# Prompt weights' transpose in the bank of the value sums, new places for the score blocks, and part of the sixth output tile ahead, in a hybrid Mamba‑2 / differential‑attention step

## The chip, the cores and the metric

The kernel runs on one core of a Trainium2 chip. The metric is the device time of one launch in microseconds (us); lower is better.

## The reference

One inference step of a two-layer diffusion backbone serves 128 prompt (context) tokens and 512 latent tokens, T = 640 together, at model width D = 1024. Layer 0 mixes tokens with a bidirectional Mamba‑2 scan, layer 1 with differential attention; after each of them comes a gated FFN with hidden width 2816 and a width-3 convolution, and a final RMSNorm ends the trunk. Every sub-layer is normalised, modulated by a conditioning vector and added back with a gate. The change touches layer 1's attention alone, which is, cut to what matters (shapes in comments, not code of the kernel):

```python
q, k, v = split(h @ w_qkv)                 # 8 heads, each two maps of 64 and values of 128
q, k = rope_2d(q), rope_2d(k)              # on latent tokens only
# prompt: 128 queries x 128 prompt keys; latent: 512 queries x (512 latent + 128 cached keys)
a0, a1 = softmax(q0 @ k0.T / 8), softmax(q1 @ k1.T / 8)
o = (a0 - lam * a1) @ v                    # per head
o = rms(o) * subg * (1 - LAM_INIT)         # norm over each head's 128 values
x = x + gate * (concat(o) @ w_ao)
```

The new keys and values of the prompt tokens are outputs too. All of it is float32.

## The kernel before

**Precision and dense tiles.** A float32 matrix product is made from two float32r parts of each operand: wh·xh, wh·xl and wl·xh. Activations lie transposed, features on 128 partitions and 640 tokens in the row. A *dense tile* is 128 output features; it goes over the inner dimension in steps k of 128, and in each step three products are made for token columns "A" (256) and "B" (384). So a step is 6 matmuls and a tile with 8 steps 48. `dense_many` (L158) issues them and calls `hook()` after every step.

**Weights.** `weight_units` lists all weight tiles in the order of their use. `nextw` takes the next one; it also starts the DMA three tiles ahead (`raw`, 4 buffers, SP's queue) and the split of the next tile: `whi` by ScalarE (helper `act`, L95) and `wlo = raw - whi` by VectorE (helper `tt`, L101). In attention there are 3 buffers of each.

**Tasks.** `hook()` advances a list of generators. A task that yields n comes back n hooks later, that is n×6 dense matmuls later. So the places of all other TensorE work among the dense matmuls are numbers in `yield`s. The framework's scheduler then decides the order on ScalarE and VectorE by priority; `high_priority()` raises that of the instructions in its block.

**PSUM.** Pool `psd` has three buffers of two banks: dense tiles (`q`, `k`, `v`, `po`) and the pairs of score tiles (`sl`, prompt: `sp`) take them in turn. Two more banks have the tags "m" (`wt`, `vt`, `ms`, `op` and, before the change, `wpt`) and "y" (`ov`).

**A head.** For each of 8 heads `attention` runs the dense tiles q, k, v. The head's scores start during its own v tile and go on in the next head's q, k and v, so tiles of one head and scores of the head before run together:
- `att_head`: prompt scores `sp`, their softmax and combination `wp`; a yield; four blocks of 128 latent queries, each 12 matmuls `sl` (both maps), a reduction `sm` on VectorE (L1079), two exponentials `e` on ScalarE, then `combine`: reciprocal, a scaling of the second map's `e` on ScalarE, and `w = e0*s + e1` on VectorE (L98). Between blocks there is a yield from a small table.
- `att_v` transposes v (`vt`, L1015) and splits it.
- `att_tail` transposes `wp` (`wpt`, L1128); then for each of five key chunks four transposes `wt` (L1145), their split `wTh` (ScalarE) and `wTl` (VectorE), and three value sums `ov` of the chunk before; then the prompt's sum `op`, squares `osq`, the row sums `ms`, nine small VectorE operations from `rs_v` (L178) to `rs_y` (`rsqrt`), and the factor back over the partitions: by DMA for heads 0 to 6, by matmul `obc` for head 7.

**The output projection.** `project_out` makes output tiles 0 to 4 over the first six heads (36 matmuls each); heads 6 and 7 finish beside it. `project_last` then adds heads 6 and 7 to tiles 0 to 4 (12 matmuls each; their weights come grouped in two units), and runs output tiles 5, 6 and 7 over all eight heads, columns A first and then B, each followed by gate, residual (`xr`) and squares for the next norm.

Of the kernel before, what the change touches and what calls it, by code (L numbers as in the profile page):

```python
# [9 lines left out]
F32 = mybir.dt.float32  # L10
# [3 lines left out]
AF = mybir.ActivationFunctionType  # L14
ALU = mybir.AluOpType
# [3 lines left out]
P = 128  # L19
D = 1024  # L20
KT = D // P
# [24 lines left out]
class Step:  # L46
# [111 lines left out]
    def dense_many(self, tiles, ks, h, parts, n=None, i0=0):  # L158


        n = n or len(ks)
        for i, k in enumerate(ks, i0):
            for ps, (hi, lo), m in tiles:
                st, sp = i == 0, i == n - 1
                wh, wl = hi[:, i * m:(i + 1) * m], lo[:, i * m:(i + 1) * m]
                for wt, x, s0, s1 in ((wh, h[k][0], st, False), (wh, h[k][1], False, False), (wl, h[k][0], False, sp)):
                    for p in parts:
                        c0, c1 = HALF[p]
                        self.mm(ps[:m, COL0[p] + c0:COL0[p] + c1], wt, x[:, c0:c1], s0, s1)
            self.hook()  # L170
# [119 lines left out]
    def project_last(self, h, ks, g, nextnorm, ks_last=None, parts="AB"):  # L290


        self.norm_begin()
        for i in range(KT - 3):
            ps = self.dense_ps("po")
            n = len(ks) * P
            j = i % (1024 // n) if ks_last else 0
            if j == 0:
                w = self.nextw()
            self.dense(ps, [t[:, j * n:(j + 1) * n] for t in w], ks, h)  # L300
            for hf in "AB":
                self.gate_add(i, ps, g, hf)
                self.norm_sq(i, hf)
        ks = ks_last or ks
        if self.modtask:
            self.drain(self.modtask)
        ws = [(self.dense_ps("po"), self.nextw(), i) for i in range(KT - 3, KT)]
        for hf in parts:
            for grp in ((ws[0:1], ws[1:3]) if hf == "B" else (ws[0:1], ws[1:2], ws[2:3])):
                self.dense_many([(ps, w, P) for ps, w, i in grp], ks, h, hf)  # L310
                for ps, w, i in grp:
                    self.gate_add(i, ps, g, hf)
                    self.norm_sq(i, hf)
            self.normt[hf] = self.add(nextnorm(hf), 3)
# [753 lines left out]
    def att_head(self, hd, qp, kp, qs, k, vs, o, pool):  # L1068


        nc = self.nc
        (qh, ql, i), (kh, kl, j) = qs, k
        lows = i, j
        half = [slice(64 * m, 64 * m + 64) for m in range(2)]

        def softmax(s, n, m, st):
            e = self.slot("f", f"e{m}", bufs=NF)
            with self.tc.high_priority():
                nc.vector.tensor_reduce(st[:, m:m + 1], s, AX.X, ALU.max, negate=True)  # L1079
                self.held["exp"] = self.act(e[:, :n], s, AF.Exp, bias=st[:, m:m + 1], accum_out=st[:, 2 + m:3 + m])  # L1080
            return e

        def stats():
            return pool.tile([P, 8], F32, tag="sm", name="sm", bufs=3)

        def combine(w, n, e0, e1, st):
            nc.vector.reciprocal(st[:, 4:6], st[:, 2:4])
            self.tt(st[:, 5:6], st[:, 5:6], self.nlam, ALU.mult)
            self.act(e1[:, :n], e1[:, :n], AF.Copy, scale=st[:, 5:6])
            self.stt(w, e0[:, :n], st[:, 4:5], e1[:, :n], ALU.mult, ALU.add)  # L1090

        r = self.psd.tile([P, 1024], F32, tag="d", name="sp")
        for m, hf in enumerate(half):
            self.mm(r[:, 512 * m:512 * m + TP], qp[hf], kp[hf], True, True)
        st = stats()
        em = [softmax(r[:, 512 * m:512 * m + TP], TP, m, st) for m in range(2)]
        yield 2
        last = hd == 7
        w = pool.tile([P, TP], F32, tag="wp", name="wp", bufs=1)
        combine(w, TP, *em, st)  # L1100
        yield 3 if last else 5 if hd else 3
        ws = []
        for b in range(4):
            qb = slice(b * P, (b + 1) * P)
            rs = [self.psd.tile([P, 1024], F32, tag="d", name="sl") for _ in range(2)]
            gate = [*self.held.values(), *lows]
            for j, (x, kk) in enumerate(((qh, kh), (qh, kl), (ql, kh))):
                for c0 in (0, 320):
                    for r, hf in zip(rs, half):
                        i = self.mm(r[:, 192 + c0:192 + c0 + 320], x[hf, qb], kk[hf, c0:c0 + 320], j == 0, j == 2)  # L1110
                        if j == 0:
                            self.hold(i, gate)
            st = stats()
            em = [softmax(r[:, 192:832], T, m, st) for m, r in enumerate(rs)]
            yield 2
            wb = pool.tile([P, T], F32, tag="w", name=f"w{b}", bufs=8)
            combine(wb, T, *em, st)
            ws.append(wb)
            if b < 3:
                yield {0: (3, 2, 2), 6: (2, 2, 2), 7: (1, 1, 1)}.get(hd, (4, 4, 4))[b]  # L1120
        self.tails[hd] = self.add(self.att_tail(hd, w, ws, vs, o, pool), 1 if last else 4)

    def att_tail(self, hd, w, ws, vs, os_, pool):

        nc = self.nc
        vh, vl, vp = vs
        pm = self.bank("m", "wpt")
        nc.tensor.transpose(pm[:, :P], w, self.ident)  # L1128
        wpT = pool.tile([P, TP], F32, tag="wpT", name="wpT", bufs=1)
        self.act(wpT, pm[:, :P], AF.Copy)  # L1130
        yield 1
        py = self.bank("y", "ov")
        o = self.slot("f", f"o{hd}", bufs=NF)
        os_.append(o)

        def av(kc, hi, lo, gate):
            self.hold(self.mm(py, vh[:, kc, :], hi, kc == 0, False), [gate])
            self.mm(py, vh[:, kc, :], lo, False, False)
            self.mm(py, vl[:, kc, :], hi, False, kc == NCH - 1)

        prev = None
        for kc in range(NCH):
            pm = self.bank("m", "wt")
            for b in range(4):
                nc.tensor.transpose(pm[:, b * P:(b + 1) * P], ws[b][:, kc * P:(kc + 1) * P], self.ident)  # L1145
            hi = pool.tile([P, TS], F32R, tag="wTh", name="wTh", bufs=2)
            lo = pool.tile([P, TS], F32R, tag="wTl", name="wTl", bufs=2)
            self.act(hi, pm, AF.Copy)
            gate = self.tt(lo, pm, hi.bitcast(F32), ALU.subtract)
            if prev:  # L1150
                av(kc - 1, *prev)
            prev = hi, lo, gate
            yield 1 if hd == 7 else 2
        av(NCH - 1, *prev)
        self.act(o[:, :TS], py, AF.Copy)
        pm = self.psm.tile([P, 512], F32, tag="m", name="op")
        self.mm(pm[:, :TP], vp, wpT, True, True)
        self.act(o[:, TS:], pm[:, :TP], AF.Copy)
        yield 1
        sq = self.slot("sq", "osq", bufs=1)  # L1160
        self.act(sq, o, AF.Square)
        yield 2
        if hd == 7:
            bc = yield from self.rms_bcast(lambda: self.wide("obc"), [sq], 0, T, P, 4)
        else:
            bc = yield from self.rms_spread(pool, [sq], P, 9)
        self.stt(o, o, self.sg[:, hd // 7:hd // 7 + 1], bc[:, :T], ALU.mult, ALU.mult)

    def attention(self, h, nextnorm, pool):
# [8 lines left out]
        for hd in range(8):  # L1178
            q, qp = self.att_evac(self.next_tile(h, "q"), hd, "q", pool)
            k, kp = self.att_evac(self.next_tile(h, "k"), hd, "k", pool)  # L1180
            nc.sync.dma_start(self.a["kout"][hd], kp)
            q = self.att_q(q, hd, pool)
            k = self.att_k(k, hd, pool)
            vs = []
            tk.append(self.add(self.att_head(hd, qp, kp, q, k, vs, o, pool), 1 if hd == 7 else 4))
            self.add(self.att_v(self.next_tile(h, "v"), hd, vs, pool), 1)
            if hd:
                self.drain(tk[hd - 1])
# [25 lines left out]
    def weight_units(self):  # L1214
        a = self.a
        u = [(a["w_dt"], 512)]
# [18 lines left out]
        for hd in range(8):  # L1235
# [3 lines left out]
        per = 1024 // (D - c)  # L1239
        u += [(a["w_ao"][i:j, :, c:].rearrange("i p c -> p i c"), (j - i) * (D - c))  # L1240
              for i in range(0, KT - 3, per) for j in (min(i + per, KT - 3),)]
        u += [(a["w_ao"][i], D) for i in range(KT - 3, KT)]
        u += ffn(1)
        return u

# [135 lines left out]
```

## Time and profile before

| what | value |
|---|---|
| median of 3 runs | 1879.43 us (1876.5 to 1879.79) |
| the profiled execution's own time | 1880.65 us |
| its span | 1878.9 us, 32832 instructions |
| TensorE (PE) busy | 1838.2 us, 98% |
| PE's weight loads (PEld) | 1741.9 us, 93% |
| VectorE (DVE) busy | 1369.5 us, 73% |
| ScalarE (ACT) busy | 952.9 us, 51% |
| mean granted TensorE clock | 0.995 |

The profile shows one execution. A timeline row gives start, duration, engine, line, operation and, in brackets, the idle time just before it with what ended it. A group gives the busy sum, the mean duration in ns and the idle time. The table of waits gives, for each kind of instruction and releaser, the idle sum, the count and the longest. The windows table gives busy time, granted clock (PEclk) and DMA share of each stretch. All helpers' instructions carry the helper's line (L95 ScalarE, L98 and L101 VectorE, L104 matmul), so they are told apart by the names of their tiles.

### The profile page before, as it was taken

How to read it: one execution, taken by the hardware profiler on the slowest of the kernel's cores; microseconds unless marked ns; L12 is line 12 of the kernel's file. 1: busy time of each engine (PE TensorE's matmuls, PEld its weight loads, DVE VectorE, ACT ScalarE, POOL GpSimd, SP SyncE). 2: the span in 40 equal slices, each digit the busy share in tenths (PEclk: the TensorE clock that was granted, in tenths of full speed). 3: DMA queues.
4: the chain of work that ended last, by engine and by line, in shares of the span. 5: the costliest groups of instructions: out<-in, count | busy, mean ns of one | idle time of the engine just before them, and what ended most of it. 6: DMA issues, size and time to landing. Idle time of an engine off the chain costs nothing.

```text
span 1878.9 us, 32832 instructions
## 1 busy us (share of the span) xinstructions
PE 1838.2 (98%) x13322; PEld 1741.9 (93%) x13322; DVE 1369.5 (73%) x2637; ACT 952.9 (51%) x1745; POOL 0.2 (0%) x4
## 2 busy tenths in 40 slices
PE   7999999999999999999999999999999999999997
PEld 5899999999999999999999988888899999999996
DVE  5699999999658999974555877788777543553554
ACT  3489687878336441441443656566445432431441
POOL 0000000000000000000000000000000000000000
PEclk9999999999999999999999999999999999999998
DMA  9835243436624556532222212111122222122211
GB/s 337 266 121 147 97 147 109 140 115 202 199 80 142 185 180 221 181 103 91 68 68 78 79 40 65 58 50 48 61 88 89 69 79 80 63 72 89 64 40 57
DMA packets 79679, 209.74 MB, mean 112 GB/s; under 512 B 9276, under 2 KB 16040, under 8 KB 79400
## 3 DMA queue, kind: packets, MB, share of 16 engines
q1 hardware_dynamic: 78952, 207.13, 33.5%
q8 instruction: 104, 1.70, 0.4%
q10 hardware_dynamic: 576, 0.52, 0.1%
q14 instruction: 47, 0.39, 0.1%
HBM read 201.66 MB, written 5.96 MB: 111 GB/s over the span
## 4 chain that ended last, share of the span: by engine, by line
PE 91%; DVE 4%; ACT 3%; DMA 1%; issue 1%; SPq 0%; DVEq 0%; ACTq 0%
PE up L104 31%; PE po L104 25%; PE z L104 6%; PE x L104 5%; PE st L104 5%; PE bc L104 3%; PE yp L104 3%; PE q L104 2%; PE v L104 2%; PE k L104 1%; PE modrow L104 1%; PE sl L104 1%; PE in L104 1%; ACT whi L95 1%; ACT e L95 1%; PE ov L104 1%
## 5 line engine op out<-in xcount | busy, mean ns | idle before, releaser
L95 ACT ACTIVATE whi<-raw 128x1024 fp32r<-128x1024 f32 (+3 forms) x227 | 234.2, 1033 | 387.2 <-PE po L104 239.6
L101 DVE TENSOR_TENSOR wlo<-raw,whi 128x1024 fp32r<-128x1024 f32 (+2 forms) x226 | 269.2, 1192 | 172.2 <-ACT whi L95 165.1
L98 DVE SCALAR_TENSOR_TENSOR xr<-po,mod,xr 128x256 f32<-128x256 f32 (+2 forms) x231 | 89.2, 433 | 162.0 <-PE po L104 161.8
L104 PE MATMUL po<-mh,whi 128*128 128x256 f32 (+1 forms) x704 | 167.8, 310 | 0.0
L104 PE MATMUL po<-ml,whi 128*128 128x256 f32 (+1 forms) x704 | 167.5, 310 | 0.0
L104 PE MATMUL po<-mh,wlo 128*128 128x256 f32 (+1 forms) x704 | 167.3, 310 | 0.0
L104 PE MATMUL up<-h11h,wlo 128*128 128x256 f32 (+1 forms) x656 | 149.4, 309 | 0.0
L104 PE MATMUL up<-h01h,wlo 128*128 128x256 f32 (+1 forms) x656 | 149.4, 308 | 0.0
L104 PE MATMUL up<-h01h,whi 128*128 128x256 f32 (+1 forms) x656 | 149.3, 308 | 0.0
L104 PE MATMUL up<-h01l,whi 128*128 128x256 f32 (+1 forms) x656 | 149.3, 308 | 0.0
L104 PE MATMUL up<-h11l,whi 128*128 128x256 f32 (+1 forms) x656 | 149.3, 308 | 0.0
L104 PE MATMUL up<-h11h,whi 128*128 128x256 f32 (+1 forms) x656 | 149.3, 308 | 0.0
L104 PEld LDWEIGHTS po<-mh,whi 128*128 128x128 f32 x704 | 128.5, 188 | 0.7 <-ACT mh L95 0.5
L104 PEld LDWEIGHTS po<-mh,wlo 128*128 128x128 f32 x704 | 128.8, 188 | 0.0
L104 PEld LDWEIGHTS po<-ml,whi 128*128 128x128 f32 x704 | 128.6, 188 | 0.0
L104 PEld LDWEIGHTS up<-h01h,whi 128*128 128x128 f32 x656 | 119.3, 188 | 0.0
L104 PEld LDWEIGHTS up<-h01h,wlo 128*128 128x128 f32 x656 | 119.3, 188 | 0.0
L104 PEld LDWEIGHTS up<-h01l,whi 128*128 128x128 f32 x656 | 119.3, 188 | 0.0
L104 PEld LDWEIGHTS up<-h11h,whi 128*128 128x128 f32 x656 | 119.2, 188 | 0.0
L104 PEld LDWEIGHTS up<-h11h,wlo 128*128 128x128 f32 x656 | 119.2, 188 | 0.1
L104 PEld LDWEIGHTS up<-h11l,whi 128*128 128x128 f32 x656 | 119.2, 188 | 0.0
L98 DVE SCALAR_TENSOR_TENSOR ca<-uraw,fcw,ca 128x511 f32<-128x511 f32 (+1 forms) x176 | 85.2, 546 | 11.6 <-ACT ca L95 11.6
(497 smaller groups left out, 4315.6 us busy)
## 6 DMA issues: line engine op xcount, KB each, us to landing
raw<-in_w_up SPq DMA_DIRECT2D x88, 512.0 KB, 3.5
mw<-in_modT SPq DMA_DIRECT2D x48, 512.0 KB, 3.5
raw<-in_w_in SPq DMA_DIRECT2D x40, 512.0 KB, 5.5
rb<-rowd SPq DMA_DIRECT2D x40, 512.0 KB, 5.6
raw<-in_w_dn SPq DMA_DIRECT2D x32, 448.0 KB, 3.2
raw<-in_w_qkv SPq DMA_DIRECT2D x24, 512.0 KB, 3.5
mr<-in_mod SPq DMA_DIRECT2D x44, 256.0 KB, 5.7
mp<-in_modp SPq DMA_DIRECT2D x32, 256.0 KB, 5.4
```

Source lines behind the costliest of these rows:

```text
L95: return self.nc.scalar.activation(out, in_, func, **k)
L98: return self.nc.vector.scalar_tensor_tensor(out, in0, s, in1, op0, op1)
L101: return self.nc.vector.tensor_tensor(out, a, b, op)
L104: return self.nc.tensor.matmul(out, lhsT, rhs, start=start, stop=stop)
```

## The change

Four edits, all inside attention:

1. `wpt` is placed in bank "y" instead of bank "m".
2. The places of score blocks change: every head but 0 starts its prompt scores one hook after its v tile is begun instead of four (head 7 did so already); the yield between the prompt's part and the first block becomes 12 for head 1, 6 for head 6 and 7 for heads 2 to 5 (5 before), and stays 3 for heads 0 and 7; the yields between the blocks become 2, 3, 5 for head 0 and 3, 3, 3 for head 1.
3. The splits `wTh` and `wTl` are issued at high priority.
4. In `project_last` the sixth output tile (number 5) is allocated first, and its columns A over heads 0 to 5 (18 matmuls) are issued ahead of tile 0's remainder; later only heads 6 and 7 are left of them. Its weights move ahead of the two grouped units in the order of loads.

```diff
     def dense_many(self, tiles, ks, h, parts, n=None, i0=0):
-        n = n or len(ks)
+        n = n or i0 + len(ks)
...
         self.norm_begin()
+        first = [(self.dense_ps("po"), self.nextw(), P)] if ks_last else []
+        self.dense_many(first, range(ks[0]), h, "A", KT)
         for i in range(KT - 3):
...
-        ks = ks_last or ks
+        ks_from, ks = ks[0], ks_last or ks
         if self.modtask:
             self.drain(self.modtask)
-        ws = [(self.dense_ps("po"), self.nextw(), i) for i in range(KT - 3, KT)]
+        ws = [(*(first[i] if i < len(first) else (self.dense_ps("po"), self.nextw()))[:2], KT - 3 + i) for i in range(3)]
         for hf in parts:
             for grp in ((ws[0:1], ws[1:3]) if hf == "B" else (ws[0:1], ws[1:2], ws[2:3])):
-                self.dense_many([(ps, w, P) for ps, w, i in grp], ks, h, hf)
+                i0 = ks_from if first and hf == "A" and grp == ws[0:1] else 0
+                self.dense_many([(ps, w, P) for ps, w, i in grp], ks[i0:], h, hf, i0=i0)
...
         combine(w, TP, *em, st)
-        yield 3 if last else 5 if hd else 3
+        yield {0: 3, 1: 12, 6: 6, 7: 3}.get(hd, 7)
...
             if b < 3:
-                yield {0: (3, 2, 2), 6: (2, 2, 2), 7: (1, 1, 1)}.get(hd, (4, 4, 4))[b]
+                yield {0: (2, 3, 5), 1: (3, 3, 3), 6: (2, 2, 2), 7: (1, 1, 1)}.get(hd, (4, 4, 4))[b]
...
-        pm = self.bank("m", "wpt")
+        pm = self.bank("y", "wpt")
...
-            self.act(hi, pm, AF.Copy)
-            gate = self.tt(lo, pm, hi.bitcast(F32), ALU.subtract)
+            with self.tc.high_priority():
+                self.act(hi, pm, AF.Copy)
+                gate = self.tt(lo, pm, hi.bitcast(F32), ALU.subtract)
...
-            tk.append(self.add(self.att_head(hd, qp, kp, q, k, vs, o, pool), 1 if hd == 7 else 4))
+            tk.append(self.add(self.att_head(hd, qp, kp, q, k, vs, o, pool), 1 if hd else 4))
...
-        u += [(a["w_ao"][i], D) for i in range(KT - 3, KT)]
+        u.insert(-2, (a["w_ao"][KT - 3], D))
+        u += [(a["w_ao"][i], D) for i in range(KT - 2, KT)]
```

## The prediction

> **What bounds the kernel now.** First the page: its busy times and the chain that ended last.
>
> ```profile
> span 1878.9 us, 32832 instructions
> PE 1838.2 (98%) x13322; PEld 1741.9 (93%) x13322; DVE 1369.5 (73%) x2637; ACT 952.9 (51%) x1745; POOL 0.2 (0%) x4
> PE 91%; DVE 4%; ACT 3%; DMA 1%; issue 1%; SPq 0%; DVEq 0%; ACTq 0%
> ```
>
> TensorE (PE) sets the time, and the change neither adds nor drops a matmul. So only PE's waits and its clock can move. I compared the queues of the two built programs, engine by engine: they have the same instructions, and their order is the same up to the second head's k tile (near 1063 us of the trace) and again after the attention output. The next views, the waits of PE from 1060 to 1360 us and the windows, therefore hold all that can be won.
>
> ```profile
> engine line waited for: us in total, times, longest us
> PE q L104 <- ACT e L95: 3.4, 6, 1.8
> PE v L104 <- ACT e L95: 2.8, 6, 0.8
> PE wpt L1128 <- DVE rs_v L178: 2.2, 5, 0.4
> PE obc L104 <- DVE rs_y L98: 1.5, 1, 1.5
> PE ov L104 <- DVE wTl L101: 1.3, 4, 0.3
> PE sl L104 <- ACT e L95: 1.2, 1, 1.2
> ```
>
> ```profile
> core 0: us, PE busy (x) PEld busy (x) DVE busy (x) ACT busy (x) POOL busy (x), PEclk, DMA share, GB/s
> 1086.00:1089.00 3.00, 3.00 (x12) 3.00 (x13) 1.21 (x3) 1.81 (x4) 0.00 (x0) 0.50 0.12 44
> ...
> 1122.00:1270.00 148.00, 141.67 (x992) 123.26 (x990) 116.28 (x235) 90.48 (x190) 0.00 (x0) 1.00 0.17 55
> ...
> 1310.00:1380.00 70.00, 67.71 (x491) 61.91 (x492) 51.47 (x110) 31.52 (x60) 0.00 (x0) 1.00 0.20 67
> ```
>
> The four steady heads (scores of heads 2 to 5) lie in 1122 to 1270 with 6.3 us idle (148 - 141.67), four waits each: q and v tiles for the exponential that frees their PSUM buffer, `wpt` for the row sums in bank "m", the last `ov` for its cast. The one stretch at half clock follows head 0's last block. These rows give my prices.
>
> ```profile
> 1072.20 0.56 PE L104 MATMUL v<-h10h,whi 128*128 128x256 f32 x2 [0.77 <-ACT e L95]
> 1082.80 0.56 PE L104 MATMUL sl<-kh,qh 64*128 64x320 f32 x4 [1.20 <-ACT e L95]
> 1083.98 1.56 DVE L1079 TENSOR_REDUCE sm<-sl 128x1 f32<-128x640 f32 x2
> 1084.84 0.79 ACT L95 ACTIVATE e<-sl,sm 128x640 f32<-128x640 f32 x1 [0.42 <-DVE sm L1079]
> 1085.78 0.90 PE L104 MATMUL q<-h10h,whi 128*128 128x256 f32 x2 [1.83 <-ACT e L95]
> 1089.08 0.45 PE L104 MATMUL q<-h10h,whi 128*128 128x256 f32 x2
> ...
> 1122.71 0.56 PE L104 MATMUL q<-h10h,whi 128*128 128x256 f32 x2 [0.24 <-ACT e L95]
> ...
> 1196.57 0.56 PE L104 MATMUL q<-h10h,whi 128*128 128x256 f32 x2 [0.31 <-ACT e L95]
> ...
> 1205.73 0.66 PE L1145 MATMUL wt<-cst,w 128*128 128x128 f32 x4
> 1206.42 0.60 ACT L95 ACTIVATE wTh<-wt 128x512 fp32r<-128x512 f32 x1 [0.75 <-PE wt L1145]
> 1207.05 0.69 DVE L101 TENSOR_TENSOR wTl<-wt,wTh 128x512 fp32r<-128x512 f32 x1 [1.17 <-ACT wTh L95]
> ...
> 1212.86 0.45 PE L104 MATMUL k<-h10h,whi 128*128 128x256 f32 x2
> 1214.61 0.60 PE L1145 MATMUL wt<-cst,w 128*128 128x128 f32 x4
> ...
> 1217.99 0.51 PE L104 MATMUL ov<-wTh,vh 128*128 128x512 f32 x1 [0.32 <-DVE wTl L101]
> ...
> 1223.10 0.33 PE L1128 MATMUL wpt<-cst,wp 128*128 128x128 f32 x1 [0.45 <-DVE rs_v L178]
> 1223.87 0.56 PE L104 MATMUL v<-h10h,whi 128*128 128x256 f32 x2 [0.45 <-ACT e L95]
> 1233.41 0.56 PE L104 MATMUL q<-h10h,whi 128*128 128x256 f32 x2 [0.34 <-ACT e L95]
> ```
>
> Twelve dense matmuls take 1.75 us (1212.86 to 1214.61), 0.146 each. From a reduction's start to its exponential it is 0.86 us (1083.98, 1084.84), from there to the tile that takes the buffer 0.94 (1085.78). From `wt` to the end of `wTl` it is 2.01 us (1205.73 to 1207.74); I take 2.06 for the PE instruction behind it. A first matmul after a wait lasts 0.56 and not 0.45, so each wait costs 0.1 more than its printed idle. The groups of the steady heads, by form, give the other durations.
>
> ```profile
> L95 ACT ACTIVATE e<-e,sm 128x640 f32<-128x640 f32 x17 | 14.0, 824 | 8.1 <-DVE sm L101 8.1
> L95 ACT ACTIVATE whi<-raw 128x1024 fp32r<-128x1024 f32 x12 | 12.7, 1055 | 7.3 <-PE k L104 5.7 <-PE q L104 1.6
> L101 DVE TENSOR_TENSOR wlo<-raw,whi 128x1024 fp32r<-128x1024 f32 x12 | 14.7, 1225 | 7.9 <-ACT whi L95 7.8
> L1079 DVE TENSOR_REDUCE sm<-sl 128x1 f32<-128x640 f32 x32 | 24.8, 816 | 6.8 <-PE sl L104 6.8
> ```
>
> **The change, part by part.** I walked through the changed program's queues with these durations; each sum is an estimate.
>
> *a. Head 0's blocks.* Head 1's v tile still starts at 1072.20. The prompt scores now come first, after 9 of its 48 matmuls, the third block after 26 (before: after 16, with the prompt scores behind it), and the last block after all 48, as before. The third block starts near 1076.7 and ends near 1077.8. On VectorE a weight split (1.2) and a rope product stand ahead of its reductions, which start near 1078.6. Two of them (1.6) and the second exponential (0.95) release the last block at about 1081.2, not 1082.80: the wait of 1.20 is gone. But v has run out, and the next q tile needs the last block's first exponential. Ahead of it in the queues stand reciprocal and product (0.35), the scaling of `e` (0.82), `whi` (1.06) and, before the reduction on VectorE, `wlo` (1.22): 1081.2 + 0.35 + 0.82 + 1.06 + 1.22 + 0.86 + 0.94 = 1086.4. That is 0.6 later than 1085.78. The two idle stretches become one of about 3.9 us.
>
> Now the clock. Before, 3.03 us of idle in two pieces (1.20 and 1.83) were followed by a granted clock of 0.50, and the first 12 q matmuls took 3.30 us (1085.78 to 1089.08) instead of 1.75: 1.55 lost. I take the same loss again; between none and double, the bounds are -1.55 and +1.55. [...] **a: +0.6.**
>
> *b. Head 1's blocks.* The last one starts after 43 of v's 48 matmuls (before: 39). On ScalarE `whi` stands ahead of its exponential and waits for v's last product with the old weights, about 0.5 us after the block; with 1.06 for `whi` the exponential starts 1.6 and the q tile 2.5 us after the block, while PE has 0.75 us of v left and the `wpt`. The wait is about 1.6 instead of the 0.24 at 1122.71, a loss of 1.4; small waits of 0.5 (`wpt` with its drain) go. **b: +0.9**, bounds 0 (`whi` finds its buffer free) and +1.4.
>
> *c. Heads 2 to 5.* The four waits of a head, 0.32 + 0.45 + 0.45 + 0.34 with 0.1 each for the restart, cost 2.0 of the 36.84 us from q to q (1196.57 to 1233.41). All four go: `wpt` finds bank "y" free since the last `ov`; the block before v and the one before q now lie early enough; the casts come at high priority. But the first hook of this order puts the second block at the end of the q tile, and the k tile that follows takes the PSUM buffer of the block. Its chain from the `wt` ahead (time A): cast to `wTl` and the next `wt` at A + 2.06; that one's `wTh` starts 0.69 later and, at high priority, stands ahead of the exponential on ScalarE for 0.6; exponential to k tile 0.94: A + 4.3. PE has 2.5 us of work meanwhile (two sets of `wt`, three `ov`, one block, the rest of q). So 0.75 is lost at the `wt` and 0.9 at the k tile: 1.65 in head 2. Head 3 adds 0.2 (its first block waits for v's evacuation behind `whi`) and 0.4 (`vt` for a `wTl`): 2.25. Heads 4 and 5 have another order: 0.2 + 0.4 + 0.5 + 0.1 + 0.9 = 2.1. Together 8.1 against 8.2 before. **c: -0.1.** Bounds: all idle of this stretch gone, -6.3; or the second rival's price.
>
> *d. Heads 6 and 7* run in other places of the same kind: head 6 loses 0.65 where it lost 1.4 (-0.7); head 7's second output tile waits 1.5 for the exponential instead of 0.70, and two small waits come (+1.0).
>
> ```profile
> 1323.02 0.56 PE L104 MATMUL po<-o0h,whi 128*128 128x256 f32 x2 [0.70 <-ACT e L95]
> 1347.55 0.48 PE L104 MATMUL ms<-osq,cst 128*32 128x160 f32 x8
> 1351.80 1.35 PE L104 MATMUL obc<-rs_y,cst 128*128 128x160 f32 x8 [1.52 <-DVE rs_y L98]
> ...
> 1369.58 1.22 DVE L101 TENSOR_TENSOR wlo<-raw,whi 128x1024 fp32r<-128x1024 f32 x1
> 1370.85 0.39 PE L104 MATMUL po<-o0h,wlo 128*128 128x256 f32 x1
> ```
>
> **d: +0.3**, bounds -0.7 and +1.0.
>
> *e. The end.* `obc` needs its factor 4.25 us after `ms` (1347.55 to 1351.80) and found 14 dense matmuls to cover that; now it has 25, which with `ms` last 4.1. So 1.4 of the 1.52 goes. The 18 matmuls ahead need head 7's scaling of `o`, which reads `obc`'s buffer; 36 matmuls (5.3 us) of output tile 4 hide that. What is late next: the seventh output tile. Its `wlo` ended at 1370.80 and its first use was at 1370.85, with no slack, although 24 matmuls of the sixth tile lay in front. With 18 of them gone there is 2.2 us less cover (18 x 0.12, columns A alone); ScalarE and VectorE get their inputs some 1 us earlier, as the tile sums end earlier, so about 1.1 is lost. The reordered DMA (512 KB ahead of two grouped units) meets a DMA share of 0.20 (1310 to 1380) and is asked for three tiles ahead: nothing. **e: -0.3**, bounds -1.4 and +0.8 (2.2 in full).
>
> Sum: 0.6 + 0.9 - 0.1 + 0.3 - 0.3 = +1.4 us. The profiled execution took 1880.65, 1.2 above the median of the runs, so it would take 1882.0, and the median 1879.43 + 1.4 = **1880.8 us**.
>
> **The rivals.** *Faster:* the new waits at the k tiles do not come, because the exponential overtakes the cast or the real latencies are shorter than my chain; then the waits named in the table simply go: 2.2 (`wpt`) + 1.3 (`ov`) + 2.8 (v) + 1.5 (`obc`) = 7.8, less a and b (1.5) and 0.4 at the seventh tile: -5.9, 1873.5. For it: every releaser on the list is moved further from its waiter. Against: the cast's 2.01 us is in the rows, and PE has only 2.5 us where 4.3 are needed. It decides at an exponential ready within 2.5 us of the `wt`.
>
> *Slower:* the pair of waits near each k tile, 0.75 and 0.9 with one set of casts between, halves the clock as the pair 1.20 and 1.83 did: four heads at 1.55 more, +6.2 on the forecast, 1887.0. For it: no gap of 3 us was needed there. Against: the `obc` gap of 1.52 had no such effect, nor had the 1.58 of idle in each steady head (clock 1.00 from 1122 to 1270). It decides at about 3 us of idle within 4.2 us of PE time. [...]
>
> *Nothing happens:* gaps only change names, 1879.4; it lies inside the forecast's own range.
>
> **How the numbers follow.** Forecast 0.55, with its own range 1876.5 to 1884.5 (c by two thirds of a wait per head, the bounds of a, b, e taken partly together); faster rival 0.25; slower rival 0.20. The range of 8 in 10 reaches to both rivals, 1873.0 to 1887.0. About 0.2% (3.8 us) is what a measurement of this kernel can tell: below 1875.7 lie 0.9 of the first rival and 0.06 of the forecast (0.26), above 1883.2 lie 0.9 of the second and 0.14 of the forecast (0.26); 0.48 is left.
>
> **What the profile after would show.** Right: no `wpt` and no `obc` wait; k tiles waiting for `e` by 0.7 to 1.0 and `wt` for `wTl` in heads 2 to 5; q to q still 36.6 to 37.1; one gap of 3.5 to 4.2 us before the q tile near 1086.4 and clock 0.50 behind it; 1.3 to 1.8 at the next q tile; a wait for `wlo` at the seventh output tile. Wrong: q to q of 35.5 or less (first rival), a clock below 1.00 within 1122 to 1270 (second), or a q tile before 1085, by which a would turn into a gain.

## The result, and the profile after

| | before | after |
|---|---|---|
| median of 18 runs | 1879.42 us (1876.5 to 1881.03) | 1882.70 us (1879.87 to 1885.87) |
| ratio to before | | 1.0020 (95% interval 1.0013 to 1.0028) |
| profiled execution, span | 1880.65, 1878.9 | 1880.28, 1878.5 |
| PE busy | 1838.2 (98%) | 1835.2 (98%) |

The change makes the kernel 3.3 us slower, at the edge of what a measurement of this kernel can tell. The forecast was +1.4, with a range that holds the result. Most of the waits that it named came; it lacked one stall of PE, which the experiments below isolate.

The two profiled executions can't be compared by their totals: code that the change does not touch ran 2.67 us faster in the execution after (the first q tile behind the start tiles begins at 1050.74 and not 1053.41). The window from 20 to 40 us shows a part of the reason; first the kernel before, then after:

```profile
20.00:40.00 20.00, 18.28 (x239) 15.32 (x235) 14.08 (x28) 7.96 (x16) 0.00 (x0) 0.91 1.01 363
```

```profile
20.00:40.00 20.00, 18.05 (x252) 15.17 (x243) 15.87 (x31) 8.66 (x16) 0.00 (x0) 1.00 1.02 360
```

A granted clock of 0.91 over 20 us is some 3.6 us at half rate (windows of 1 us show 0.51, 0.50 and 0.50 from 24 to 27 us and 0.78 in the next), or 1.8 lost, which one execution had and the other had not. So I compare a stretch: from that first q tile to the first `up` tile of the next FFN. It took 362.59 us before (1053.41 to 1416.00) and 364.55 after (1050.74 to 1415.29), +1.96; three more executions of the changed kernel gave 365.50, 366.79 and 366.02. The mean of the four is 3.1 above the one execution of before, close to the medians' +3.3. That one execution has a scatter too: the kernel with only the early sixth tile (below) runs the instructions of before up to the last q tile, and took 218.00 us from the first q tile to there, before 216.88.

The waits of PE after, from 1060 to 1360 us:

```profile
engine line waited for: us in total, times, longest us
PE q L104 <- ACT e L95: 4.8, 2, 3.3
PE k L104 <- ACT e L95: 4.5, 4, 1.5
PE wt L1148 <- DVE vl L101: 2.3, 3, 1.6
PE po L104 <- ACT e L95: 1.6, 2, 1.3
PE wt L1148 <- DVE wTl L101: 1.2, 3, 0.5
PE vt L1018 <- DVE wTl L101: 0.9, 2, 0.5
```

`wpt` and `obc` are gone from the list, v has 0.3 left of 2.8, and k and `wt` have come in their place: the gaps changed their names. The PE timeline after shows where they lie:

```profile
1083.36 0.56 PE L104 MATMUL q<-h10h,whi 128*128 128x256 f32 x2 [3.28 <-ACT e L95]
1121.74 0.56 PE L104 MATMUL q<-h10h,whi 128*128 128x256 f32 x2 [1.52 <-ACT e L95]
1130.04 0.66 PE L1148 MATMUL wt<-cst,w 128*128 128x128 f32 x4 [1.62 <-DVE vl L101]
1136.42 0.66 PE L1148 MATMUL wt<-cst,w 128*128 128x128 f32 x4 [0.50 <-DVE wTl L101]
1138.53 0.56 PE L104 MATMUL k<-h10h,whi 128*128 128x256 f32 x2 [0.76 <-ACT e L95]
1212.93 0.56 PE L104 MATMUL k<-h10h,whi 128*128 128x256 f32 x2 [1.49 <-ACT e L95]
1324.69 0.57 PE L104 MATMUL po<-o0h,whi 128*128 128x256 f32 x2 [1.29 <-ACT e L95]
1350.84 1.25 PE L104 MATMUL obc<-rs_y,cst 128*128 128x160 f32 x8
1370.59 0.39 PE L104 MATMUL po<-o0h,wlo 128*128 128x256 f32 x1 [1.02 <-DVE wlo L101]
```

The wait of 1.62 is not in the prediction. `vl` is the low part of the split of v; it reads `vt` in bank "m", which the next `wt` takes. VectorE's timeline after shows what stood before `vl`: the scaling of a finished head, waiting for the DMA that brings its factors.

```profile
1128.50 0.88 DVE L98 SCALAR_TENSOR_TENSOR o<-o,sg,rbc 128x640 f32<-128x640 f32 x1 [2.07 <-DMA rbc<-rsd]
1129.30 0.68 DVE L101 TENSOR_TENSOR vl<-vt,vh 128x512 fp32r<-128x512 f32 x1
```

In the kernel before, `vl` came first at this place, and the scaling behind it had nothing to wait for:

```profile
1128.60 0.68 DVE L101 TENSOR_TENSOR vl<-vt,vh 128x512 fp32r<-128x512 f32 x1
1129.20 0.88 DVE L98 SCALAR_TENSOR_TENSOR o<-o,sg,rbc 128x640 f32<-128x640 f32 x1
```

So two things came together: `vl` and the scaling swapped places in VectorE's queue, and the DMA landed late. SP's queue shows what goes with the late landing. Before, the factors were asked for ahead of the next weight load:

```profile
1126.00 0.33 SPq L217 DMA_DIRECT2D rbc<-rsd  x1
1127.25 0.33 SPq L125 DMA_DIRECT2D raw<-in_w_qkv  x1
```

After, 512 KB of weights are asked for first:

```profile
1122.81 0.33 SPq L125 DMA_DIRECT2D raw<-in_w_qkv  x1
1123.23 0.38 SPq L217 DMA_DIRECT2D rbc<-rsd  x1
```

From issue to landing `rbc` took up to 4.0 us before and up to 5.2 after (all eleven transfers of the kernel; before, then after).

```profile
DMA to landing us min/median/max: 3.0/3.2/4.0
```

```profile
DMA to landing us min/median/max: 3.0/3.6/5.2
```

In the first trace of the changed kernel, the two scalings that waited for an `rbc` asked for 0.4 us behind a weight load began 5.3 and 4.6 us after its issue (1123.23 to 1128.50, 1198.75 to 1203.34); in the trace of before, where no `rbc` comes that close behind a load, the three that waited began 3.3 to 3.4 us after it. No run moved the transfer itself, so that the load ahead of it is the cause is likely but not shown.

### The profile page after: what moved, and what is told of

Same layout as the page of the kernel before. It is cut to its first block, busy times and chain, and to the rows that moved or that the text cites. A ratio compares the mean times of both kernels' runs of the same rounds, so it can differ in the third digit from the quotient of the medians.

```text
span 1878.5 us, 32838 instructions
## 1 busy us (share of the span) xinstructions
PE 1835.2 (98%) x13322; PEld 1740.6 (93%) x13322; DVE 1367.9 (73%) x2637; ACT 954.4 (51%) x1745; POOL 0.2 (0%) x4
## 4 chain that ended last, share of the span: by engine, by line
PE 89%; DVE 5%; ACT 3%; DMA 2%; issue 1%; SPq 0%; DVEq 0%; ACTq 0%
PE up L104 31%; PE po L104 25%; PE z L104 6%; PE x L104 5%; PE st L104 5%; PE bc L104 3%; PE yp L104 3%; PE k L104 2%; PE q L104 2%; ACT e L95 1%; PE v L104 1%; PE modrow L104 1%; PE ov L104 1%; PE sl L104 1%; DVE wlo L101 1%
## 5 line engine op out<-in xcount | busy, mean ns | idle before, releaser
L95 ACT ACTIVATE whi<-raw 128x1024 fp32r<-128x1024 f32 (+4 forms) x227 | 234.3, 1033 | 388.2 <-PE po L104 235.1
```

The lines of the kernel that those rows point to most:

```text
L95: return self.nc.scalar.activation(out, in_, func, **k)
```

## The experiments

**The changed kernel again, three times.** The kernel is the same; the question is what differs between its executions.

> The changed kernel once more, to see another of its executions. Theory (the queues decide): the new waits are fixed by the order of the queues, so from the first q tile after the start tiles to the last st tile of the next FFN the second trace needs the same time within 0.5 us as the first (351.95), the ratio to before is again 1.002 (+3 to +4 us), and what differs between executions lies before that stretch. Rival (the clock): the spread of 6 us between executions goes with a granted clock of 0.994 to 0.996; an execution of 1883 us or more then shows a further stretch at half clock inside the attention, at one of the new gaps, worth 1.5 us each.

Measured: median 1882.96, ratio 1.0014 (1.0006 to 1.0023), 3.2 us above the runs of before beside it. The traced execution had no further half clock, but 365.50 in the stretch: 0.95 more than the first, nearly all of it at one place, where a `wt` waited 1.16 for `vl` and not 0.25, because `rbc` landed later. So the stretch is not fixed within 0.5, and this trace did not speak for the clock.

> The changed kernel in a third traced execution. Theory (most of the difference between executions of one kernel is the clock, in pieces of 3.4 us at half rate, and the landing of rbc): an execution above 1882.5 shows a second piece of 3.4 us behind the gap at head 1's end, or one near 20 to 40 us of the start, or waits of wt for vl above 1.8 us; one near 1880 shows none of them. Rival: the time differs in stretches in which neither changes.

> The changed kernel in a fourth traced execution; the same as for the third.

Measured: 1883.41 and 1881.57 us, 366.79 and 366.02 in the stretch. Both have a second piece of half clock, right behind the wait for `vl`; the third has the piece between 20 and 40 us as well (granted clock 0.91 there), the fourth has not (1.00). PE timeline and windows of the third execution:

```profile
1123.96 0.56 PE L104 MATMUL q<-h10h,whi 128*128 128x256 f32 x2 [1.52 <-ACT e L95]
1132.88 0.74 PE L1148 MATMUL wt<-cst,w 128*128 128x128 f32 x4 [2.25 <-DVE vl L101]
```

```profile
1125.00:1133.00 8.00, 5.75 (x44) 5.08 (x43) 4.28 (x10) 3.42 (x8) 0.00 (x0) 1.00 0.35 109
1133.00:1136.00 3.00, 3.00 (x14) 3.00 (x15) 1.58 (x3) 1.31 (x2) 0.00 (x0) 0.55 0.00 0
1136.00:1140.00 4.00, 4.00 (x27) 3.16 (x26) 1.38 (x2) 1.82 (x3) 0.00 (x0) 0.91 0.06 16
```

A clock of 0.55 over 3 us and 0.91 over 4 is 2.7 + 0.7 = 3.4 us at half rate, 1.7 us lost. In the two executions with a wait of 1.62 and 1.77 there it did not happen, in the two with 2.13 and 2.25 it did; four executions don't fix a threshold. This is the slower rival's mechanism at another place than the rival had it.

**Each part alone.** Only the yields:

```diff
-        yield 3 if last else 5 if hd else 3
+        yield {0: 3, 1: 12, 6: 6, 7: 3}.get(hd, 7)
...
-                yield {0: (3, 2, 2), 6: (2, 2, 2), 7: (1, 1, 1)}.get(hd, (4, 4, 4))[b]
+                yield {0: (2, 3, 5), 1: (3, 3, 3), 6: (2, 2, 2), 7: (1, 1, 1)}.get(hd, (4, 4, 4))[b]
...
-... 1 if hd == 7 else 4))
+... 1 if hd else 4))
```

> Only the yields and the start of the prompt scores are changed; wpt stays in bank m, casts and projection as before. Theory (the places of the blocks cost, the other parts give a little back): slower than before by 3 to 5 us, with k tiles waiting 0.7 to 1.5 for e, q of the fourth head by about 1.5, and obc by 1.5. Rival (the bank move is what brings the new waits, as it lets wt and ov start elsewhere): within 1 us of before, with no k wait over 0.3.

Measured: 1879.66, ratio 0.9999 (0.9991 to 1.0008). The theory's size was wrong, and so was the rival's "no k wait": the k waits are all there (5.2 us in four), and to the last head's q tile the kernel is 1.8 us behind. But from there to `up` it gains 2.7: `obc` finds its factor ready without any other part of the change (1.52 before), and a wait of 1.13 for the squares of the next norm is gone as well. The wait for `vl` is here too, 1.28 at `wpt`, with the scaling in front of `vl` waiting 1.46 for `rbc`: so the places brought that stall.

Only the bank:

```diff
-        pm = self.bank("m", "wpt")
+        pm = self.bank("y", "wpt")
```

> Only wpt goes to bank y. Theory: the wpt waits (2.2 us in five) go, but the v tile just behind waits for an exponential whose time does not depend on wpt, so its wait grows by what wpt no longer takes: v waits rise from 2.8 to about 4.5 and the time is within 1 us of before (-0.5). Rival (waits simply vanish): -2.2 to -2.8 us.

Measured: 1877.64, ratio 0.9988 (0.9979 to 0.9997), 2.1 us below the runs of before beside it (1879.75), where -0.5 was expected. In the steady heads it went as the theory said: the v tile takes over what `wpt` gave up, and no `wt` waits more than 0.2 for `vl`.

```profile
1147.16 0.56 PE L104 MATMUL v<-h10h,whi 128*128 128x256 f32 x2 [0.96 <-ACT e L95]
```

That was 0.45 for `wpt` and 0.44 for v before; q to q is 36.8 to 37.1, as before. The gain of this kernel too comes from the end: the stretch from the last q tile to `up` is 2.6 us shorter, without the waits of 1.52 and 1.13. So the number is near the rival's and the mechanism is not, and places and bank each earn the same 2.6 us. No kernel has these two alone together; the sum further down says that they can be earned once.

Only the early sixth tile (edit 4 of the change):

> Only the sixth output tile's columns A for the first six heads go ahead, with the order of its weights. Theory: obc's 1.52 goes, a wait of about 1.0 for wlo comes at the seventh output tile and part of it is given back at the next norm's sums: -0.5 (0 to -1.2). Rival (the cast has slack after all): no wlo wait, -1.4; other rival (the new order stalls earlier, at head 7's scaling): +0.5 or more.

Measured: 1880.14, ratio 1.0003 (0.9994 to 1.0012). The expectation failed at its first step: `obc` still waits 1.51, so the early tile is not what took its wait away; the wait for `wlo` of 1.02 came as expected. From the last q tile to `up` it is 0.7 slower.

**The changed kernel without one part.**

> The changed kernel without the part on the sixth output tile (bank, places and priority stay). Theory (the early columns A cost more than they hide: 1.02 at the seventh tile's wlo, 0.35 at the next norm's sums and two restarts, while obc has no wait either way): about 1.6 us faster than the changed kernel, so +1.4 to before (1881.2), with no wlo wait after obc and obc still without a wait. Rival (the early tile is what took obc's wait away): obc waits by 1 us or more again and the time stays at +3.

Measured: 1882.54, ratio 1.0014 (1.0005 to 1.0023), 3.6 us above the runs of before beside it and not 1.4. Both waits behaved as the theory says (no `wlo`, no `obc`), and from the last q tile to `up` it was 1.0 us shorter than the changed kernel, not 1.6; the medians do not show it.

```diff
-            with self.tc.high_priority():
-                self.act(hi, pm, AF.Copy)
-                gate = self.tt(lo, pm, hi.bitcast(F32), ALU.subtract)
+            self.act(hi, pm, AF.Copy)
+            gate = self.tt(lo, pm, hi.bitcast(F32), ALU.subtract)
```

> The changed kernel without the high priority of the wTh and wTl casts. Theory (the casts stand in the same order nearly everywhere, as the built queues differ only in heads 6 and 7): within 1 us of the changed kernel (+2.3 to +4.0 to before), k tiles still wait 0.76 to 1.5 for e. Rival (casts ahead of exponentials make the k waits): k waits below 0.3 and 3 us faster than the changed kernel.

Measured: 1880.35, ratio 1.0009 (1.0000 to 1.0018), 1.4 us above the runs of before beside it, so the theory's +2.3 to +4.0 was missed. The k waits are unchanged (4.5 us in four), so the rival falls too. But the part is not idle: without it the output tile that waited 1.29 waits 0.46, and from the last q tile to `up` the time is 1.5 shorter. With the priority, `whi`, which itself waits 0.92 for PE, and a `wTh` stand ahead of that tile's exponential on ScalarE; without it `whi` comes behind.

With 145.6 us from the last q tile to `up`, the changed kernel is as long as before (145.7): by this sum of single traces, the 2.6 that bank or places earn, less the 1.0 of the early tile and the 1.5 of the priority.

**The stall that was missing.** VectorE's scaling of a finished head is issued three hooks later and made to come behind `vl`:

```diff
-        self.tt(flat(lo), pm, flat(hi).bitcast(F32), ALU.subtract)
+        self.vlg = self.tt(flat(lo), pm, flat(hi).bitcast(F32), ALU.subtract)
...
-            bc = yield from self.rms_spread(pool, [sq], P, 9)
-        self.stt(o, o, self.sg[:, hd // 7:hd // 7 + 1], bc[:, :T], ALU.mult, ALU.mult)
+            bc = yield from self.rms_spread(pool, [sq], P, 12)
+        i = self.stt(o, o, self.sg[:, hd // 7:hd // 7 + 1], bc[:, :T], ALU.mult, ALU.mult)
+        if hd < 6:
+            self.hold(i, [self.vlg])
```

> The changed kernel with one thing moved: VectorE's scaling of a finished head (o times rbc, which waits for the DMA that brings the factors) is queued behind the split vl of the value tile, for heads 0 to 5. Theory (the rbc transfer lands later because a 512 KB weight load now stands before it in SP's queue, VectorE waits for it 0.7 to 2.2 us, vl stands behind, and wt behind vl): the waits of wt for vl of 1.62 and 0.25 to 1.16 go, 2.0 to 2.8 us faster than the changed kernel, so +0.5 to +1.3 to before, and the scatter of the runs shrinks. Rival (the next wait takes over: wt would have waited for its w or for a bank anyway): less than 0.7 us faster.

Measured: 1878.77, ratio 0.9998 (0.9989 to 1.0007): the whole loss is gone. Against the runs of before beside each, this kernel stands at -0.2 and the changed kernel at +3.3; that is 3.5 us, more than the 2.0 to 2.8 expected. The one trace says less: 363.50 from the first q tile to `up`, 1.0 to 3.3 below the four traces of the changed kernel. It has no half clock between 1105 and 1275 us, as two of those four have; how much of the 3.5 is that, one trace can't say. Nor is the scatter shown to shrink: 11 runs lie within 4.0 us, 11 of the changed kernel within 4.2 (the first repetition above). VectorE and PE of this kernel at the same place:

```profile
1129.47 0.69 DVE L101 TENSOR_TENSOR vl<-vt,vh 128x512 fp32r<-128x512 f32 x1 [0.71 <-ACT vh L95]
1130.29 0.60 PE L1148 MATMUL wt<-cst,w 128*128 128x128 f32 x4
1131.56 0.89 DVE L98 SCALAR_TENSOR_TENSOR o<-o,sg,rbc 128x640 f32<-128x640 f32 x1 [1.40 <-DMA rbc<-rsd]
1133.37 0.33 PE L1024 MATMUL vt<-cst,v 128*128 128x128 f32 x1 [1.00 <-DVE wTl L101]
```

`wt` no longer waits, but the scaling still waits for `rbc`: the cast `wTl` now stands behind it, and the next `vt` waits 1.00 for that cast. So a part of the stall is left; from q to q head 2's scores take 36.95 here and took 37.97 to 39.93 in the changed kernel. The k waits remain (3.7 us in four) and have moved: 1.41 in head 2, and 0.76 in heads 4 and 5, where the changed kernel had 1.49.

**What the rule is worth.** If a dense tile waits for a block that lies too near, blocks further from the tiles should pay. On the bank move alone:

```diff
-...get(hd, (4, 4, 4))[b]
+...get(hd, (4, 2, 3))[b]
```

> Only the bank of wpt from the change, and the yields between the blocks of heads 1 to 5 as 4, 2, 3 instead of 4, 4, 4, so that every block lies at least 18 dense matmuls ahead of the next dense tile. Theory (a dense tile waits for the exponential of a block that lies within about 2.8 us before it): the v waits of 0.96 and q waits of 0.31 of the bank-only kernel fall to 0.3 or less together, in 5 heads, and no k wait comes: 3 to 5 us faster than bank alone, -5 to -7 to before (1873 to 1875). Rival (blocks closer together: VectorE and ScalarE become the limit and the waits go to wt for w): within 1 us of bank alone.

Measured: 1872.45, ratio 0.9967 (0.9955 to 0.9980), 4 to 5 us below the bank alone, as the theory said. v, q and k waits of the steady heads are gone, and q to q falls from 36.8 or more to 34.9; some 0.45 at the prompt scores `sp` is left in each. At the end it gives 3.3 us back: from the last q tile to `up` it takes 146.47, the bank alone 143.15, with two output tiles waiting 1.47 and 1.46 and the next norm's squares 1.29. And for the gap at head 1's end, head 0's yields:

```diff
-{0: (3, 2, 2), ...
+{0: (2, 2, 1), ...
```

> The kernel with the bank move and blocks at 4, 2, 3, and head 0's yields between blocks 2, 2, 1 instead of 3, 2, 2: its last block comes 27 matmuls into head 1's v tile and not after all 48. Theory (the q tile after head 1's v waits because the weight split and two reductions stand between the last block and its exponential while PE has nothing left, and the half clock is the price of that long gap): the 1.09 and 2.57 of idle become at most 1.5 together, no granted clock of 0.50 follows, 4 to 6 us faster than the kernel with bank and 4, 2, 3 (1867 to 1869). Rival (VectorE is full in these 26 us, so the same idle comes in other places): less than 1.5 us faster, still 3.4 us at half clock.

Measured: 1869.14, ratio 0.9939 (0.9925 to 0.9952): 11 us faster than before and 13 to 15 than the changed kernel. It is 3.3 below the last kernel by the medians and 4.8 against the runs of before beside each (4 to 6 expected). The q tile has no wait left and the half clock behind it is gone, as the windows of this kernel show beside those of the kernel before in the prediction (0.50 from 1086 to 1089; 141.67 busy of 148):

```profile
1083.00:1090.00 7.00, 6.61 (x51) 6.02 (x50) 4.98 (x12) 4.71 (x11) 0.00 (x0) 1.00 0.23 77
1090.00:1122.00 32.00, 31.68 (x227) 28.58 (x225) 25.47 (x55) 21.82 (x47) 0.00 (x0) 1.00 0.12 40
1122.00:1270.00 148.00, 145.93 (x1048) 129.89 (x1049) 119.81 (x239) 93.06 (x197) 0.00 (x0) 1.00 0.20 60
```

The rival (VectorE full in these 26 us) falls: what held the q tile was the order, not the load.

## Why the prediction was right, and where it was not

By its own steps, in the traced pair:

| step | forecast | measured | where |
|---|---|---|---|
| a, head 0's blocks | +0.6 | +0.25 | to the q tile after head 1's v (32.37, 32.62) |
| b, head 1's blocks | +0.9 | +1.45 | from that q to the next (36.93, 38.38) |
| c, heads 2 to 5 | -0.1 | +0.36; +2.7 in the third execution, +1.7 in the mean of the four | the next four q to q (147.58, 147.94, 150.31) |
| d and e, the rest | 0.0 | -0.10 | from the last q tile to `up` (145.71, 145.61) |

**a** held: the two idle stretches became one, 3.28 us long (forecast 3.9), and the half clock came again, as the windows after show: 0.04 + 0.50 x 3 + 0.17 below full rate, again 3.4 us at half rate (before, the windows of 1 us from 1085 to 1089 show 0.79, 0.50, 0.50 and 0.51).

```profile
1083.00:1084.00 1.00, 0.64 (x4) 0.64 (x5) 0.38 (x2) 1.00 (x5) 0.00 (x0) 0.96 0.90 348
1084.00:1087.00 3.00, 3.00 (x13) 3.00 (x12) 1.21 (x3) 1.40 (x3) 0.00 (x0) 0.50 0.11 38
1087.00:1088.00 1.00, 1.00 (x9) 0.98 (x8) 0.00 (x0) 0.00 (x0) 0.00 (x0) 0.83 0.00 0
```

**b** had the wait right (1.52; 1.6 was forecast) and the total 0.55 too low. I had credited 0.5 of small waits that go; the timeline before has only 0.21 there, at one `wt`. The stretch holds the same matmuls but for one `wpt`, and the q tile's are busy for 9.61 us and not 9.35, as all of the half clock falls on them.

**c** is the step that failed, by one term that it lacked. The waits that it named came, most of them smaller: 0.50 at `wt` and 0.76 at the k tile of head 2 (0.75 and 0.9 forecast); 1.25 in head 3, where 2.25 stood; 1.9 in heads 4 and 5 (2.1), but 1.49 of it at the k tile, where 0.9 stood. Together they are 6.4 us in the first trace, and 8.1 was forecast; the sum also charges 0.1 for each restart before the change and none after it. What it lacked is the wait of `wt` for `vl`, 1.87 in that trace. So the first trace's +0.36 is close to -0.1 by luck, as two errors nearly cancel, and q to q came out 36.2 to 38.0, not 36.6 to 37.1.

The chain of c follows PE, ScalarE and VectorE and names no DMA: the scaling that waits for `rbc`, in VectorE's queue ahead of `vl`, is not in it, and the new order of loads was weighed for the output weights alone (step e). The term is worth 1.6 to 2.25 at head 2, 0 to 1.16 at head 4, and 1.7 for the clock in two of four executions. With the scaling moved the kernel ties with before, and that is shown. It stands at -0.2, though, and not at the +1.4 that was forecast without this stall: the named terms were too high, as the 6.4 for 8.1 says, and the k waits of heads 4 and 5 went down as well.

**d and e** came out right in sum, and partly by luck. `wlo` (1.02, forecast 1.1), `po` (1.29, forecast 1.5) and the vanished `obc` wait are as forecast. But the factor is ready in time through the places or the bank alone, the early tile gains nothing that the runs show, and in the changed kernel the wait of 1.29 comes with the high priority, which has no price in d. A second wait, 1.13 for the squares of the next norm before and 0.35 after, is not in the prediction.

**The rivals.** The faster one needed k tiles without waits and fell. The slower one named the right price, half a clock's loss, and the wrong place: the pair 0.50 and 0.76 never halved the clock in four executions; 1.52 and 2.13 to 2.25, 9 us apart, did. The idle time before it does not give the length of the half clock either: the longest gap of the changed kernel, 3.26 to 3.29 us at head 1's end, was followed by 3.4 us at half rate in all four executions, and the pair 1.20 and 1.83 there by 3.4 us in one trace (before) and 6.8 in another (the early sixth tile alone; last section).

## What to carry to other kernels

When a reordering removes a wait, follow the queue of each engine to the next instruction that has nothing to do with it, and ask of every instruction ahead of it whether it waits for a DMA; a transfer that lay ahead of a weight load in the issuing queue may now lie behind one. Moving work away from a tile's start pays only if it does not move to the next tile's start: here blocks 18 or more matmuls ahead of each boundary gained 4 to 5 us, and trading one boundary for another gained nothing. The 18 is a place that worked and not a measured limit: in the changed kernel v tiles 12 matmuls behind a block did not wait, and head 1's, 18 behind, waited 0.33. Look at the same stretch of code in several executions before comparing totals.

## What the runs showed of the hardware that was not expected

Half clock came in whole pieces. Added up from windows of 1 us between 1080 and 1100, the time at half rate behind head 1's end was 3.4 us in nine of the twelve traces of kernels with that gap and 6.8 in three. Two traces with identical instructions up to there (before, and the early sixth tile alone) had 3.4 and 6.8: the first 18 q matmuls took 4.27 and 5.10 us, and the second was 1.25 us later at the next k tile. In the one trace with no gap of 1 us there it was zero. Pieces of the same length near 20 to 40 us, in code that no kernel here changes, go with the start of attention: the first q tile began at 1050.74 and 1052.16 in the two executions with a granted clock of 1.00 from 20 to 40 us (the changed kernel's first and fourth), and at 1053.41 and 1053.04 in the two with 0.91 (before, and the changed kernel's third). 1.7 us of that is the clock; the rest was not followed.
